# Later side steps in a two-block float32 kernel: the mixer's and the stick-breaking heads', with joined first loads

## The chip, the cores and the metric

One core of one Trainium2 chip runs the whole program. The metric is the device time of one execution in microseconds (us). Three runs of the kernel before gave 2051.86, 2054.35 and 2055.33 us: a median of 2054.35. Lower is better. Everything is float32.

## What is computed

A sequence of 256 rows with 2048 columns goes through two blocks. The first has a state-space mixer, a layer norm, a sparse-attention mixer and a layer norm. The second has an attention of two kinds of heads and an MLP. Only two pieces matter here. The mixer (64 groups of 16 channels, 64 complex states each):

```python
def s5_mixer(x, w_in, ...):
    u, z = jnp.split(x @ w_in, 2, axis=-1)
    ...
    bu_r = jnp.einsum('lbgc,gpc->lbgp', ug, bbar_r)
    _, _, h_r, h_i = lax.associative_scan(_complex_linear_combine, (ar, ai, bu_r, bu_i), axis=0)
    y = einsum('gcp,lbgp->lbgc', c_re, h_r) - einsum('gcp,lbgp->lbgc', c_im, h_i)
    y = y + d_skip * u
    g = jax.nn.gelu(y)
    y = g * jax.nn.sigmoid(g @ w_glu + b_glu)
    return (y * jax.nn.silu(z)) @ w_out
```

And the second block's stick-breaking heads (8 of them, 128 wide):

```python
z = einsum("bqhd,bkhd->bhqk", qb, k) * scale
log_one_minus = jnp.where(strict, jax.nn.log_sigmoid(-z), 0.0)
log_stick = lax.cumsum(log_one_minus, axis=3, reverse=True) - log_one_minus
a = jnp.where(strict, jnp.exp(jax.nn.log_sigmoid(z) + log_stick), 0.0)
out = einsum("bhqk,bkhd->bqhd", a, v)
```

Their outputs are normalised per head, joined with 8 differential heads and multiplied with `w_out` (`co` and `cp` in the profile).

## The kernel before

TensorE (PE) runs one long row of weight chunks. A chunk is a product of the 256 rows with a slice of a weight matrix, 16 k slices of 128 deep, one k slice a step. Beside it go smaller jobs, written as Python generators ("streams"). After each k slice, `step` advances every stream by one, so what a stream does lands between two k slices of the running chunk. `later(n, f)` is a stream that sleeps n steps and then calls f. `drain` runs all streams to their end with nothing between. The instructions go to the engines in the order of the calls, except that a scheduler may still move those not marked `in_order`.

**The mixer.** `u_chunk(b)` (b from 0 to 3) and then `z_chunk(b)` are products with 256 columns of `a_w_in`, full float32, two matmuls (128x256) a k slice (`plain_chunk`, L106 and on; L120). 16 copies on ScalarE (ACT, L394) bring a finished u into `ug`. The states go in four quarters b, each with steps registered by `beside(b)` (L706):

- `b_powers` (L560 to L580, on VectorE, DVE, and ACT's L593): powers of the decay times the input weights, into `ybuf`.
- `states` (L647): 32 PE products `S<-ug,xbuf`, then a DVE chain of 12 pieces from L667 through two scans (L674) to `Hp` (L677, L678).
- `input_weights` (L608): 16 PE transposes `w1t`, four ACT copies (L616) into `W1`.
- `next_c`: the output weights' powers on DVE. `c_blocks` (L600): ACT copies of them into `CP0` and `CPk`.
- `lags` (L621): 32 PE products `tt`, on DVE a copy into `Kl` (L637, L639), then a round trip through DRAM on POOL's queue: `kd` (L642), and four DMAs (L644) into `Tt`.
- `within` (L682): 16 PE products `yb<-ug,Tt`. `outputs` (L690): 32 PE products `yb<-Hp,CPk` into the same bank, then 16 Gelus on ACT (L699).

Between the chunks stands a `drain()`. The buffer `xbuf` holds x (8192 elements a partition: 4096 of x, then W1 and the second CPk). The first chunk's x goes there by 6 DMAs on SyncE's (SP) queue, its weights by 6 DMAs on ACT's queue, into `r_in`.

**The second block.** For each half of the heads, `attend` (L1248) is a stream beside the chunks dv, the queries and keys, `v`, and what follows `v` (`d` in half 0, `co` in half 1). For the stick-breaking heads `weights` is `stick_weights` (scores `sc`, ACT, DVE and POOL, last L1246 on POOL into `lb`). `turned` (L1162) transposes `lb` on PE (`wT`, L1165), `weigh` (L1170) multiplies with the values (`ob`, L1174 to L1176) once the chunk `v` has left PSUM through `sv` (L1151 on ACT, two pieces). `head_out` squares `ob` on ACT, takes a root on DVE, writes `mo` (L1187), transposes it (`moT`, L1193) and stores it as `yH` (ACT) and `yL` (DVE).

Of the kernel before, what the change touches and what calls it, by code (L numbers as in the profile page):

```python
# [17 lines left out]
P = 128  # L18
# [10 lines left out]
def fused_blocks(ctx: ExitStack, tc, ins, out, dbg=None, stages="ABCD"):  # L29
# [318 lines left out]
    with tc.tile_pool(name="pa", bufs=1) as pa:  # L348
# [39 lines left out]
        def u_chunk(b):  # L388
            bank = plain_chunk(ins["a_w_in"][b], xraw, f"u{b}", *((8, 8), space, nc.sync) if b else ((1, 1, 2, 4, 4, 4), first_space, nc.scalar))
# [6 lines left out]
        def z_chunk(b):  # L396
            bank = plain_chunk(ins["a_w_in"][4 + b], xraw, f"z{b}", (8, 8), space, nc.sync)
# [18 lines left out]
        Tt = pa.tile([P, 8, P], F32, name="Tt")  # L416
        G.memset(Tt, 0.0)
# [124 lines left out]
        def rotation(b):  # L542
# [13 lines left out]
               xbuf[:, 6144:8192].rearrange("p (q r k c) -> p q r k c", q=8, r=2, k=4)]  # L556
        for t in CP0 + CPk:
            n = math.prod(t.shape[1:])
            A.copy(t.rearrange("p q r c -> p (q r c)" if len(t.shape) == 4 else "p q r k c -> p (q r k c)"),
                   zero.to_broadcast([P, n]))  # L560
# [39 lines left out]
        def c_blocks(b):  # L600
            cx = cxs[:, b]
            for g in range(2):
                gs, gc = halves(g)
                A.copy(CP0[b % 2][gs, :, :, gc], cx[gs])
                A.copy(CPk[b % 2][gs, :, :, :, gc].rearrange("p q r k c -> p k (q r) c"),
                       Call[gs].rearrange("p k q r c -> p k (q r) c"))

        def input_weights(half):  # L608
            for q2 in (2 * half, 2 * half + 1):
# [6 lines left out]
                A.copy(W1[:, 2 * q2:2 * q2 + 2].rearrange("p q r s -> p (q r s)"), bank)  # L616
# [119 lines left out]
        gHL = big.tile([P, 8, 2, S], F32R, tag="yH", name="gHL")
        gH, gL = gHL[:, :, 0, :], gHL[:, :, 1, :]
        gT = ug.rearrange("p b (m t) -> p (b m) t", m=2)
        for m in range(0, 8, 2):
            A.copy(gH[:, m:m + 2, :], gT[:, m:m + 2, :])  # L740
            V.tensor_sub(gL[:, m:m + 2, :], gT[:, m:m + 2, :], gH[:, m:m + 2, :].bitcast(F32))
        z_chunk(2)
# [7 lines left out]
        for c in range(4):  # L750
            pair = wide_chunk(ins["a_w_glu"][c], (gH, gL, gHL), f"glu{c}")
# [290 lines left out]
    with tc.tile_pool(name="pc", bufs=1) as pc:  # L1042
# [127 lines left out]
        def weigh(wT, v, h, ob):  # L1170
# [3 lines left out]
            T.matmul(ob[:, o:o + P], lhsT=wT[:, 0:128], rhs=v[:, 0, hs], start=(h % 2 == 0), stop=True, skip_group_check=True)  # L1174
# [74 lines left out]
        def attend(weights, q, k, v, norm, k0, gap, wait, first):  # L1249
# [136 lines left out]
def lay_out(i):  # L1386
# [5 lines left out]
    a["xt"] = xt.reshape(P, KD, S)  # L1392
# [18 lines left out]
    a["a_w_in"] = _tiles(i["a_w_in"][0], 8, 256)  # L1411
    a["a_w_glu"] = _tiles(i["a_w_glu"][0], 8, 256)
# [53 lines left out]
```

## Time and profile before

| | us |
|---|---|
| median of three runs | 2054.35 |
| the profiled execution | 2057.24 |
| its span in the trace | 2055.4 |
| PE busy (matmuls) | 2009.5, 98% |
| DVE busy | 1235.4, 60% |
| ACT busy | 935.4, 46% |
| mean granted TensorE clock | 0.991 of full |

The times of instructions count from the start of the span. Busy time is the union of an engine's instructions, so a PE that is 98% busy still may do its work at half the clock: the column PEclk of the windows gives the clock that was granted (1.00 is 2.4 GHz, 0.50 is 1.2 GHz). A full-float32 matmul leaves two records where a cheaper one leaves one. A wait is put down to the semaphore that came last.

### The profile page before, as it was taken

Reading aid. Unit: us, or ns where it says so; the run is one execution under the profiler, and the core shown is the slowest. Engines: PE = TensorE matmul, PEld = TensorE weight load, DVE = VectorE, ACT = ScalarE, POOL = GpSimd, SP = SyncE. Lnnn points to the kernel's source line nnn. Section 1 sums busy time; section 2 is a strip of 40 time slices with the busy share of each in tenths; the row PEclk is TensorE's granted clock in tenths of the full one; section 3 lists DMA queues with packets and bytes.
Section 4 is the critical chain, followed back from the end, with each engine's and each line's share of the span. In section 5 each row is a group of like instructions: output and inputs, shape, how many; then the busy total and the mean of one; then the engine's idle time right before and its main releaser. Section 6 shows DMA issues by size and latency. Waiting matters only on the chain.

```text
span 2055.4 us, 27590 instructions
## 1 busy us (share of the span) xinstructions
PE 2009.5 (98%) x11376; PEld 1708.0 (83%) x11376; DVE 1235.4 (60%) x1802; ACT 935.4 (46%) x1223; POOL 76.0 (4%) x117
## 2 busy tenths in 40 slices
PE   8899999999999999999999999999999999999997
PEld 7788788888888888877878887888888888888886
DVE  8755764466666667567665665565455555555554
ACT  5543543345444545346565565444334334433443
POOL 0110200000000000020010011000000000000000
PEclk9999999999999999999999999999999999999999
DMA  8334554544545454554544544555555555555553
GB/s 313 94 123 153 205 186 166 185 159 167 171 144 175 153 185 144 185 196 176 173 161 144 173 154 154 174 206 185 202 187 186 195 190 187 189 198 186 189 198 124
DMA packets 57119, 361.52 MB, mean 176 GB/s; under 512 B 8481, under 2 KB 9953, under 8 KB 14881
## 3 DMA queue, kind: packets, MB, share of 16 engines
q1 hardware_dynamic: 55296, 355.83, 50.4%
q10 hardware_dynamic: 864, 2.10, 0.3%
q8 instruction: 89, 1.46, 0.3%
q0 software_dynamic: 832, 1.84, 0.3%
q14 instruction: 38, 0.30, 0.0%
HBM read 357.11 MB, written 2.62 MB: 175 GB/s over the span
## 4 chain that ended last, share of the span: by engine, by line
PE 81%; DVE 2%; ACT 2%; issue 1%; POOL 1%; DMA 0%; ACTq 0%; DVEq 0%; POOLq 0%
PE mo L170 17%; PE mi L139 12%; PE bz L139 9%; PE mi L142 6%; PE bz L142 4%; PE bo L170 4%; PE co L170 4%; PE v L170 3%; PE s L139 3%; PE q L139 3%; PE d L170 2%; PE kvv L170 2%; PE kvk L139 1%; PE kvc L139 1%; PE q L142 1%; PE s L142 1%
## 5 line engine op out<-in xcount | busy, mean ns | idle before, releaser
L139 PE MATMUL mi<-hW,h_mi 128*128 128x512 f32 x1024 | 279.5, 394 | 0.0
L103 DVE TENSOR_TENSOR l_mi<-r_mi,h_mi 128x2048 fp32r<-128x2048 f32 x64 | 146.7, 2293 | 152.5 <-ACT h_mi L102 152.5
L103 DVE TENSOR_TENSOR l_mo<-r_mo,h_mo 128x2048 fp32r<-128x2048 f32 x64 | 146.7, 2292 | 149.9 <-ACT h_mo L102 149.9
L139 PE MATMUL bz<-hW,h_bz 128*128 128x512 f32 x768 | 224.3, 412 | 0.0
L102 ACT CAST h_mi<-r_mi 128x2048 fp32r<-128x2048 f32 x64 | 122.3, 1911 | 209.2 <-PE mi L139 166.9
L102 ACT CAST h_mo<-r_mo 128x2048 fp32r<-128x2048 f32 x64 | 122.4, 1913 | 202.9 <-PE mo L170 164.3
L170 PE MATMUL mo<-h_mo,yH 128*128 128x512 f32 x512 | 199.3, 389 | 0.8 <-DVE xres L1366 0.8
L170 PE MATMUL mo<-h_mo,yL 128*128 128x512 f32 x512 | 199.3, 389 | 0.0
L170 PE MATMUL mo<-l_mo,yH 128*128 128x512 f32 x512 | 199.3, 389 | 0.0
L139 PEld LDWEIGHTS mi<-hW,h_mi 128*128 128x128 f32 x1024 | 175.3, 189 | 23.7
L142 PEld LDWEIGHTS mi<-hW,l_mi 128*128 128x128 f32 x1024 | 157.1, 189 | 21.7
L142 PE MATMUL mi<-hW,l_mi 128*128 128x256 f32 x1024 | 163.0, 281 | 0.0
L102 ACT CAST h_bz<-r_bz 128x2048 fp32r<-128x2048 f32 x48 | 91.6, 1909 | 150.3 <-PE bz L139 80.3
L103 DVE TENSOR_TENSOR l_bz<-r_bz,h_bz 128x2048 fp32r<-128x2048 f32 x48 | 110.0, 2292 | 73.7 <-ACT h_bz L102 73.7
L139 PEld LDWEIGHTS bz<-hW,h_bz 128*128 128x128 f32 x768 | 133.5, 189 | 18.4
L142 PEld LDWEIGHTS bz<-hW,l_bz 128*128 128x128 f32 x768 | 117.2, 188 | 16.6
L142 PE MATMUL bz<-hW,l_bz 128*128 128x256 f32 x768 | 121.7, 280 | 0.0
L170 PEld LDWEIGHTS mo<-h_mo,yH 128*128 128x128 f32 x512 | 96.1, 188 | 20.8 <-DVE xres L1366 1.3
L170 PEld LDWEIGHTS mo<-h_mo,yL 128*128 128x128 f32 x512 | 96.1, 188 | 20.1
L170 PEld LDWEIGHTS mo<-l_mo,yH 128*128 128x128 f32 x512 | 96.1, 188 | 20.0
L170 PE MATMUL d<-h_d,hW 128*128 128x512 f32 x256 | 87.6, 415 | 4.6 <-DVE hW L284 2.9
L170 PE MATMUL v<-h_v,hW 128*128 128x512 f32 x256 | 83.3, 397 | 0.0
(509 smaller groups left out, 3783.7 us busy)
## 6 DMA issues: line engine op xcount, KB each, us to landing
r_mi<-in_w_mlp_in SPq DMA_DIRECT2D x64, 1024.0 KB, 4.9
r_mo<-in_w_mlp_out SPq DMA_DIRECT2D x64, 1024.0 KB, 4.9
r_bz<-in_b_w_in SPq DMA_DIRECT2D x48, 1024.0 KB, 4.9
r_q<-in_b_w_in SPq DMA_DIRECT2D x16, 1024.0 KB, 4.9
r_bo<-in_b_w_out SPq DMA_DIRECT2D x16, 1024.0 KB, 4.9
r_d<-in_w_in_2t SPq DMA_DIRECT2D x16, 1024.0 KB, 5.0
r_v<-in_w_in_2t SPq DMA_DIRECT2D x16, 1024.0 KB, 4.8
r_s<-in_w_in_2f SPq DMA_DIRECT2D x16, 1024.0 KB, 4.9
```

Source lines behind the costliest of these rows:

```text
L102: A.copy(wh[:, a:a + w], raw[:, a:a + w])
L103: (eng or V).tensor_tensor(wl[:, a:a + w], raw[:, a:a + w], wh[:, a:a + w].bitcast(F32), op=OP.subtract)
L139: T.matmul(pair[:, m, :], lhsT=wh[:, kk, ms], rhs=aW[:, k, :, :].rearrange("p a t -> p (a t)"), start=(k == 0), stop=(k == kt - 1), skip_g ...
L142: T.matmul(pair[:, m, S:], lhsT=wl[:, kk, ms], rhs=aH[:, k, :], start=False, stop=(k == kt - 1), skip_group_check=True)
L170: T.matmul(banks[t][:, :cols], lhsT=at[:, k, ts_], rhs=wt[:, kk, :], start=(k == 0 and i == 0), stop=(k == kt - 1 and i == 2))
```

## The change

It has five parts.

1. x and the first chunk's weights are one array `xu` (16 k slices of 256 + 256 columns), loaded by 6 DMAs on SP (256 KB twice, 512 KB, 1 MB three times) straight into `xbuf`, now [128, 16, 512]. W1 and the second CPk take the weights' place in it once they are used. The ACT queue issues no load.
2. `Tt` is cleared first, and four products of its zeros (128x256, "still") stand first on PE.
3. The mixer's steps come 8 to 9 k slices later and run on into the next chunk: the drain between chunks is gone, one stands behind `z_chunk(2)`. `b_powers` is a step at 7. `lags(b+1)` now comes between `within(b)` and `outputs(b)`, before it came behind `outputs(b)`. The split of the mixer's result (`gHL`) is a step of `z_chunk(2)`.
4. ACT's copies of the powers and of W1 are pinned with `in_order`, and so is the clearing of the second CPk, now a step. `c_blocks` makes two copies of 64x512 in place of one of 64x1024.
5. The stick-breaking group sleeps two steps more before its first `turned`, four more before its first `weigh`; `turned`'s first transpose and `weigh`'s first product are pinned.

```diff
-        for size in sizes:
-            raw = space(k0, size)
-            in_order(queue.dma_start(raw, w[k0 // kk_n][:, k0 % kk_n:k0 % kk_n + size, :].rearrange("p k c -> p (k c)")))
+        for size in sizes:
+            wt = space(k0, size)
+            if load:
+                in_order(nc.sync.dma_start(wt.rearrange("p k c -> p (k c)"), ...))
...
+        Tt = pa.tile([P, 8, P], F32, name="Tt")
+        G.memset(Tt, 0.0)
+        for _ in range(4):
+            T.matmul(bank_of("pre", "still")[:, 0:256], lhsT=Tt[:, 0, :], rhs=Tt[:, 0:2, :].rearrange("p a b -> p (a b)"),
+                     start=True, stop=True)
...
         def first_space(k0, n):
             ks = slice(k0, k0 + n)
-            fetch(xraw[:, ks, :], ins["xt"][:, ks, :])
-            ...
+            fetch(xbuf[:, ks, :], ins["xu"][:, ks, :])
+            return xbuf[:, ks, S:]
...
+        def clear_second():
+            in_order(A.copy(xbuf[:, 8:16, S:], zero[:, None].to_broadcast([P, 8, 256])))
...
-                A.copy(CP0[b % 2][gs, :, :, gc], cx[gs])
-                A.copy(CPk[b % 2][gs, :, :, :, gc].rearrange("p q r k c -> p k (q r) c"),
-                       Call[gs].rearrange("p k q r c -> p k (q r) c"))
+                in_order(A.copy(CP0[b % 2][gs, :, :, gc], cx[gs]))
+                for r in range(2):
+                    in_order(A.copy(CPk[b % 2][gs, :, r, :, gc].rearrange("p q k c -> p k q c"), Call[gs, :, :, r, :]))
...
-                A.copy(W1[:, 2 * q2:2 * q2 + 2].rearrange("p q r s -> p (q r s)"), bank)
+                in_order(A.copy(xbuf[:, 2 * q2:2 * q2 + 2, S:], bank.rearrange("p (q s) -> p q s", q=2)))
...
         def beside(b):
             if b < 3:
-                b_powers(b + 1)
-            later(1, lambda: states(b))
+                later(7, lambda: b_powers(b + 1))
+            later(9, lambda: states(b))
             if b < 3:
-                later(6, lambda: input_weights(0))
-                later(8, lambda: next_c(b + 1))
-                later(9, lambda: input_weights(1))
-                later(11, lambda: c_blocks(b + 1))
-                later(14, lambda: lags(b + 1))
-            later(10, lambda: within(b))
-            later(13, lambda: outputs(b))
+                later(14, lambda: input_weights(0))
+                later(16, lambda: next_c(b + 1))
+                later(17, lambda: input_weights(1))
+                later(19, lambda: c_blocks(b + 1))
+                later(22, lambda: lags(b + 1))
+            later(18, lambda: within(b))
+            later(22, lambda: outputs(b))
...
         for b in range(4):
-            drain()
             beside(b)
             if b < 2:
                 u_chunk(b + 2)
             else:
                 z_chunk(b - 2)
+        later(10, split_output)
+        z_chunk(2)
         drain()
...
-            yield from sleep(gap)
+            yield from sleep(gap if first else gap + 2)
...
+                if not h and not first:
+                    yield from sleep(4)
                 if h % 2 == 0:
                     ob = small_bank("ob")
                 weigh(wT, v[0], h, ob)
```

What follows on the engines, at three places.

PE, the first quarter from `within(0)` on. `yb<-ug,Tt` is `within`, `yb<-Hp` is `outputs`, `tt` is `lags(1)`; `u` are the chunk's matmuls, here two a k slice. Before:

```order
89 L120 MATMUL u_524<-xbuf,r_in_606 128x256 x2
90 L232 MATMUL yb<-ug,Tt 64x64 [waits DMASW2_49,DMASW1_49]
91 L120 MATMUL u_524<-xbuf,r_in_606 128x256 x2
92 L232 MATMUL yb<-ug,Tt 64x64 [waits DMASW4_49,DMASW3_49]
93 L232 MATMUL yb<-ug,Tt 64x64 x14
94 L120 MATMUL u_524<-xbuf,r_in_606 128x256 x4
95 L232 MATMUL yb<-Hp,CPk 64x64 [waits DVE_49,Pool_49]
96 L232 MATMUL yb<-Hp,CPk 64x64
97 L232 MATMUL yb<-Hp,CPk 64x64 [waits DVE_49]
98 L232 MATMUL yb<-Hp,CPk 64x64 x29
99 L120 MATMUL u_524<-xbuf,r_in_606 128x256 x2
100 L631 MATMUL tt<-CP_299,ybuf 32x32 [waits Activation_49]
```

Now:

```order
94 L617 MATMUL w1t<-ident,ybuf 128x128 [waits Activation_49]
95 L617 MATMUL w1t<-ident,ybuf 128x128 x3
96 L121 MATMUL u_642<-xbuf,r_in_643 128x256 x2
97 L233 MATMUL yb<-ug,Tt 64x64 [waits DMASW2_49,DMASW1_49]
98 L233 MATMUL yb<-ug,Tt 64x64 [waits DMASW4_49,DMASW3_49]
99 L233 MATMUL yb<-ug,Tt 64x64 x14
100 L121 MATMUL u_642<-xbuf,r_in_643 128x256 x8
101 L636 MATMUL tt<-CP_299,ybuf 32x32 [waits PE_49,Activation_49]
102 L640 MATMUL tt<-xbuf,ybuf 32x96 [waits Activation_49]
```

The 32 products `tt` now stand ahead of the 32 products `yb<-Hp`, and 8 matmuls of the chunk instead of 4 to 6 stand between the two kinds of `yb`. Between the last `S` and the first `yb<-ug,Tt` stand 18 chunk matmuls and 16 `w1t` in both.

DVE, from `Kl` of quarter 0 (L639; now L644) to the first piece on `S` (L667; now L672). `rot` and `a` are the rotation, `ybuf`, `bcx` and `ptmp` the powers. Before:

```order
167 L639 SCALAR_TENSOR_TENSOR Kl<-id_165,dT,Kl 128x32 [waits DMAHW4_49,DMAHW1_49,DVE_49]
168 L536 TENSOR_TENSOR a_386<-rot,esg 128x512 [waits DVE_49]
169 L539 TENSOR_TENSOR rot<-rot,esg 128x2x8x32
170 L639 SCALAR_TENSOR_TENSOR Kl<-id_165,dT,Kl 128x32
171 L540 TENSOR_TENSOR rot<-rot,a_386 128x2x8x32 [waits DVE_49]
172 L539 TENSOR_TENSOR rot<-rot,esg 128x2x8x32
173 L667 TENSOR_TENSOR tA<-S_531,rot 128x512 [waits DVE_49,PE_49]
```

Now, from the third piece behind `Kl` on:

```order
174 L582 TENSOR_TENSOR bcx<-bcx,aki 128x32x16
175 L542 TENSOR_TENSOR rot<-rot,a_651 128x2x8x32 [waits DVE_49]
176 L582 TENSOR_TENSOR bcx<-bcx,aki 128x32x16
177 L592 TENSOR_TENSOR ybuf<-bcx,ccr 128x256 [waits Activation_49]
178 L541 TENSOR_TENSOR rot<-rot,esg 128x2x8x32
179 L594 TENSOR_TENSOR ybuf<-ybuf,ptmp 128x256 [waits DVE_49]
180 L541 TENSOR_TENSOR rot<-rot,esg 128x2x8x32
181 L576 TENSOR_TENSOR ybuf<-ybuf,akr 128x768 [waits DVE_49]
182 L582 TENSOR_TENSOR bcx<-ybuf,aki 128x24x16 x2
183 L593 TENSOR_TENSOR ptmp<-bcx,pt_262 128x256
184 L585 TENSOR_TENSOR ybuf<-ybuf,bcx 128x768 [waits DVE_49]
185 L672 TENSOR_TENSOR tA<-S_551,rot 128x512 [waits PE_49]
```

The next quarter's powers, which before stood behind or inside the chain from `S` to `Hp`, now stand ahead of it: 14 pieces between the last `Kl` and the first on `S`. The 12 pieces of the chain itself then follow each other without a piece between.

ACT, where `v` of the stick-breaking heads' half 0 ends. `sv` are the two pieces that empty `v` (L1151; now L1163), `lb` the weights of head 2 (L1245; now L1260). Before:

```order
533 L1151 ACTIVATE sv<-v_8693,rmy 128x512 [waits PE_49]
534 L1245 ACT_TABLE_LOAD
535 L1245 ACTIVATE lb<-lb 128x384 [waits Pool_49]
536 L1151 ACTIVATE sv<-v_8693,rmy 128x512
537 L102 CAST h_d_2_9007<-r_d_2_9005 128x2048 [waits DMAHW7_49]
```

Now:

```order
541 L1163 ACTIVATE sv<-v_8701,rmy 128x512 [waits PE_49]
542 L1163 ACTIVATE sv<-v_8701,rmy 128x512
543 L102 CAST h_d_2_8958<-r_d_2_8956 128x2048 [waits DMAHW1_49]
544 L1260 ACT_TABLE_LOAD
545 L1260 ACTIVATE lb<-lb 128x384 [waits Pool_49]
```

The second piece of `sv` no longer stands behind head 2's exponential, which waits for POOL. On PE the first `wT` of the group moves from 18 matmuls before the end of `v` to 6 before it, and the first `ob` from 6 matmuls behind the end of `v` to 30.

## Rows read from the trace of the kernel before

**Rows 1.** PE's waits over the span; us in total, times, longest.

```profile
PE ob L1176 <- ACT sv L1151: 6.5, 2, 3.7
PE u L120 <- DMA xbuf<-in_xt: 5.3, 2, 4.5
PE wT L1165 <- POOL lb L1246: 3.5, 2, 2.7
PE yb L232 <- DMA Tt<-kd: 3.1, 1, 3.1
PE yb L232 <- DVE Hp L677: 2.3, 1, 2.3
PE w1t L612 <- ACT ybuf L593: 1.6, 1, 1.6
PE ob L1174 <- ACT sv L1151: 1.1, 1, 1.1
```

**Rows 2.** PE timeline from the start: start, us, line, count, idle before.

```profile
4.53 3.85 PE L120 MATMUL u<-xbuf,r_in 128*128 128x256 f32 x8 [4.53 <-DMA xbuf<-in_xt]
9.10 22.51 PE L120 MATMUL u<-xbuf,r_in 128*128 128x256 f32 x92 [0.72 <-DMA xbuf<-in_xt]
```

**Rows 3.** Durations (ns) of the first chunk's matmuls, 10 to 12 us.

```profile
L120 PE MATMUL u<-xbuf,r_in x6: 631/631/631, 9.7 to 11.8; 128*128 128x256 f32 x6
```

**Rows 4.** The same, 12 to 16 us.

```profile
L120 PE MATMUL u<-xbuf,r_in x15: 379/379/631, 11.8 to 15.9; 128*128 128x256 f32 x15
```

**Rows 5.** Windows: PE, PEld, DVE, ACT, POOL busy, PEclk, DMA, GB/s.

```profile
0.00:10.00 10.00, 4.75 (x10) 3.19 (x11) 6.14 (x50) 5.21 (x5) 3.13 (x10) 1.00 0.79 247
10.00:20.00 10.00, 10.00 (x38) 8.30 (x37) 5.48 (x43) 2.18 (x5) 0.00 (x0) 1.00 0.95 343
59.11:66.19 7.08, 7.08 (x44) 5.30 (x45) 7.08 (x13) 0.00 (x0) 0.00 (x0) 0.57 0.01 2
91.53:96.62 5.09, 4.83 (x69) 4.12 (x69) 3.31 (x5) 1.84 (x6) 0.00 (x0) 0.66 0.01 3
1080.43:1086.45 6.02, 6.02 (x16) 4.83 (x17) 2.29 (x1) 1.73 (x1) 0.18 (x1) 0.56 0.19 27
1239.96:1243.20 3.24, 3.24 (x10) 2.68 (x10) 1.47 (x1) 1.74 (x1) 0.17 (x1) 0.56 0.00 0
```

**Rows 6.** POOL timeline at the start.

```profile
0.77 0.95 POOL L417 MEMSET Tt<- 128x1024 f32 x1
```

**Rows 7.** DVE timeline, quarter 0: first and next to last piece from S to Hp.

```profile
49.65 0.67 DVE L667 TENSOR_TENSOR tA<-S,rot 128x512 f32<-128x512 f32 x1
59.28 0.67 DVE L677 TENSOR_TENSOR Hp<-tB,tA 128x512 f32<-128x512 f32 x1
```

**Rows 8.** ACT timeline: the 16 copies that empty a u chunk.

```profile
45.23 4.27 ACT L394 COPY ug<-u 32x128 f32<-32x128 f32 x16
```

**Rows 9.** DMA landings, 60 to 80 us: KB each, us to landing.

```profile
kd<-Kl POOLq DMA_DIRECT2D x1, 128.0 KB, 5.1
Tt<-kd POOLq DMA_DIRECT2D x1, 96.0 KB, 2.6
```

**Rows 10.** DMA landings, 40 to 60 us.

```profile
Tt<-kd POOLq DMA_DIRECT2D x1, 96.0 KB, 6.5
```

**Rows 11.** PE timeline: the chunk's matmuls from the end of tt(0) on.

```profile
39.59 2.86 PE L120 MATMUL u<-xbuf,r_in 128*128 128x256 f32 x12
```

**Rows 12.** POOL timeline, stick-breaking half 1.

```profile
1226.70 2.68 POOL L1244 TENSOR_TENSOR lb<-lb,ck 128x256 f32<-128x256 f32 x1
```

**Rows 13.** ACT timeline, stick-breaking half 1: second piece of sv.

```profile
1239.24 0.67 ACT L1151 ACTIVATE sv<-v,rmy 128x512 f32<-128x512 f32 x1
```

**Rows 14.** PE timeline, last stick-breaking group: last ob, first moT.

```profile
1270.17 0.39 PE L1176 MATMUL ob<-sv,wTs 128*128 128x128 f32 x2
1277.26 0.60 PE L1193 MATMUL moT<-ident,mo 128*128 128x128 f32 x4
```

**Rows 15.** DVE timeline, the same place.

```profile
1274.22 1.12 DVE L1187 SCALAR_TENSOR_TENSOR mo<-ob,hry,hn 128x128 f32<-128x128 f32 x4
```

More of the change, by code (lines that the diff above doesn't have):

```diff
@@ L104, in load, with plain_chunk @@
         return (wh.rearrange("p (k c) -> p k c", c=cols), wl.rearrange("p (k c) -> p k c", c=cols))
-    def plain_chunk(w, x, name, sizes, space, queue):
+    def plain_chunk(w, x, name, sizes, space, load=True):
         _, _, kk_n, cols = w.shape
@@ L388, in u_chunk @@
         def u_chunk(b):
-            bank = plain_chunk(ins["a_w_in"][b], xraw, f"u{b}", *((8, 8), space, nc.sync) if b else ((1, 1, 2, 4, 4, 4), first_space, nc.scalar))
+            bank = plain_chunk(ins["a_w_in"][b], xraw, f"u{b}", *((8, 8), space) if b else ((1, 1, 2, 4, 4, 4), first_space, False))
             for q in range(4):
@@ L555, in fused_blocks @@
         CPk = [pa.tile([P, 8, 2, 4, 32], F32, name="CPk"),
[L556 to L560, printed above, removed]
+               xbuf[:, 8:16, S:].rearrange("p q (r k c) -> p q r k c", r=2, k=4)]
+        for t in CP0:
+            A.copy(t.rearrange("p q r c -> p (q r c)"), zero.to_broadcast([P, 512]))
+        A.copy(CPk[0].rearrange("p q r k c -> p (q r k c)"), zero.to_broadcast([P, 2048]))
+        def clear_second():
+            in_order(A.copy(xbuf[:, 8:16, S:], zero[:, None].to_broadcast([P, 8, 256])))
         Hp = pa.tile([P, 2, 8, 65], F32, name="Hp")
@@ L726, in fused_blocks, with split_output @@
         later(14, lambda: lags(0))
+        later(15, clear_second)
         u_chunk(1)
+        gT = ug.rearrange("p b (m t) -> p (b m) t", m=2)
+        g = []
+        def split_output():
+            gHL = big.tile([P, 8, 2, S], F32R, tag="yH", name="gHL")
+            gH, gL = gHL[:, :, 0, :], gHL[:, :, 1, :]
+            g.extend((gH, gL, gHL))
+            for m in range(0, 8, 2):
+                A.copy(gH[:, m:m + 2, :], gT[:, m:m + 2, :])
+                V.tensor_sub(gL[:, m:m + 2, :], gT[:, m:m + 2, :], gH[:, m:m + 2, :].bitcast(F32))
         for b in range(4):
-            drain()
             beside(b)
@@ L734, in fused_blocks @@
                 z_chunk(b - 2)
+        later(10, split_output)
+        z_chunk(2)
         drain()
[L736 to L742, printed above, removed]
         z_chunk(3)
@@ L750, in fused_blocks @@
         for c in range(4):
-            pair = wide_chunk(ins["a_w_glu"][c], (gH, gL, gHL), f"glu{c}")
+            pair = wide_chunk(ins["a_w_glu"][c], g, f"glu{c}")
             m0 = 2 * c
@@ L1164, in turned @@
             for i in range(3):
-                T.transpose(tb[:, i * P:(i + 1) * P], wt[:, i * P:(i + 1) * P], ident)
+                m = T.transpose(tb[:, i * P:(i + 1) * P], wt[:, i * P:(i + 1) * P], ident)
+                if i == 0:
+                    in_order(m)
             wT = pc.tile([P, 384], F32, tag="wT", name="wTs", bufs=2)
@@ L1173, in weigh @@
             o = h % 2 * S
-            T.matmul(ob[:, o:o + P], lhsT=wT[:, 0:128], rhs=v[:, 0, hs], start=(h % 2 == 0), stop=True, skip_group_check=True)
+            in_order(T.matmul(ob[:, o:o + P], lhsT=wT[:, 0:128], rhs=v[:, 0, hs], start=(h % 2 == 0), stop=True,
+                              skip_group_check=True))
             T.matmul(ob[:, o + P:o + S], lhsT=wT[:, 128:256], rhs=v[:, 0, hs], start=False, stop=False, skip_group_check=True)
@@ L1411, in lay_out @@
     a["a_w_in"] = _tiles(i["a_w_in"][0], 8, 256)
+    a["xu"] = np.concatenate([xt.reshape(P, KD, S), a["a_w_in"][0].transpose(1, 0, 2, 3).reshape(P, KD, 256)], 2)
     a["a_w_glu"] = _tiles(i["a_w_glu"][0], 8, 256)
```

20 lines of the change are left out of this document (7 added, 13 removed).

## The prediction

> **What bounds the kernel now.** I read the page first: PE is busy for 2009.5 of 2055.4 us, so 45.9 us of the span are all that PE stands still, and nothing else can be bound but PE itself. Then PE's waits by what ended them [rows 1]. The reader is to see that six of the seven rows lie in two places that the change touches: the mixer (w1t, both yb) and the stick-breaking heads (wT, both ob), and that the seventh is the start. Then the windows behind the longest waits [rows 5]: PE is busy in them, but its granted clock is 0.56 to 0.66 in the mean, between its two levels of 1.2 and 2.4 GHz. So a long wait is paid twice: for itself, and for the work behind it at half the clock. Waits of about 1 us brought no fall of the clock, those of 2.3 to 3.7 us did. Last the start [rows 2 to 4].
>
> About 0.2% (4 us) is what a measurement of this kernel can tell from no change.
>
> **Mixer waits.** They are 1.6 (w1t, behind an ACT copy), 3.1 (yb on Tt) and 2.3 us (yb on Hp) [rows 1], together 7.0. Behind the second the window of 7.08 us ran at 0.57, so (1 - 0.57) x 7.08 = 3.0 us were lost, behind the third (1 - 0.66) x 5.09 = 1.7 [rows 5]. In all 11.7 us. The change takes their causes away thus:
>
> - w1t waited for a copy that stood behind the 16 copies of u (4.27 us) [rows 8]. w1t stood 6 k slices behind the start of a chunk, now 14.
> - yb on Tt: Tt(0) landed 6.5 us after its issue, while weight loads ran [rows 10]; in the next quarter it was 2.6, though kd took 5.1 [rows 9]. tt(0) stays where it was, within(0) comes 8 k slices later: 8 x 0.92 us = 7.4, more than the 3.1 that lacked. (A k slice is two matmuls, four records; twelve records and the tail of the last take 2.86 us [rows 11].) In the later quarters tt comes earlier against yb, by the 32 products on Hp and one k slice.
> - yb on Hp: the chain of 12 pieces from S takes 59.28 + 0.67 - 49.65 = 10.3 us with three foreign pieces in it [rows 7], some 9.4 without. There is now more PE work between the two kinds of yb: 8 matmuls (3.7 us) and tt (1.1) where 4 to 6 stood.
>
> **What new waits the mixer gets.** Quarter 0 is the tight one. I walk PE through the new order with the durations of the trace: tt(0) ended at 39.59 [rows 11] and now ends 1.3 earlier (the start, below), at 38.3. 22 matmuls (10.1) and S(0) (2.0) follow, so S(0) is done at 50.4. Then 18 matmuls (8.3), w1t (1.8), yb on Tt (1.1), 8 matmuls (3.7) and tt (1.1), so PE wants tt(1) done at 66.3 and then Hp(0). On DVE Kl(0) ends at about 49.6, 14 pieces of powers of 0.33 to 0.87 us follow (about 7.9), then the chain, 9.4: Hp at 66.9. That is 0.6 late. tt(1) wants ACT's copies of c_blocks(1); u2 ends at 56.8, ACT has its 16 copies [rows 8] to about 61.3, two W1 copies, then about 3 us of c_blocks: 65.4 to 65.7, where PE comes at 65.2. I take 1.2 us of new waits in the mixer in all, none long enough for the clock. Bounds: 0 (all hidden), and 13 (the first rival). The larger number of ACT copies in c_blocks costs nothing else: ACT is idle over half of both windows behind the mixer's waits [rows 5]. The clearing of the second CPk moves behind the first chunk on ACT, covered by the same idle time.
>
> **Stick-breaking heads.** The waits are 6.5 + 3.5 + 1.1 = 11.1 us [rows 1], and at half clock behind the two longest (1 - 0.56) x 6.02 = 2.6 and (1 - 0.56) x 3.24 = 1.4 [rows 5], so 15.1. wT waits for POOL, whose piece L1244 took 2.68 us in half 1 [rows 12]; the two more steps of sleep put 12 matmuls (12 x 0.227 = 2.7 us) ahead of wT, as much as its longest wait. The second ob waited for the second piece of sv, which stood behind an exponential that waits for POOL, and in half 1 began at 1239.24 only [rows 13]. Now both pieces stand ahead of that exponential, and PE comes to ob 30 matmuls (6.8 us) after v instead of 6 (1.4). sv needs about 1.4 us in all. I let all 15.1 go; bounds 15.1 and 0 (second rival).
>
> **What is late next.** The whole group ends later, above all the last in half 1: behind its last ob stood 30 matmuls before moT wanted mo [rows 14]. mo was begun 1274.22 - 1270.56 = 3.7 us after the last ob, and the first of its four pieces was ready 0.3 later, at 4.0 [rows 14, 15]. Now 16 matmuls (3.6 us) stand between, then the four transposes with one matmul between each two, and behind 4 more and 12 to 18 others PE wants yH and yL. I put 0.7 us on it; 0 if the scheduler's order hides it, 3 if it turns into a wait that lets the clock fall.
>
> **The start.** Before, PE begins at 4.53, stands 0.72 us for data [rows 2], and its matmuls take 631 ns until 11.8, then 379 [rows 3, 4]: a pitch of 0.46 and of 0.23 us. 14 records fell into the slow part, which cost 14 x 0.23 = 3.2 us. The zero products can begin once Tt is cleared, at 0.77 + 0.95 = 1.7 us [rows 6], and take 8 records of 0.46: to 5.5. Weights and x come by one queue, but need no more than what the traffic gave: 2.47 MB in the first 10 us and 3.43 in the next [rows 5], so 4.2 MB are there at 15, and the chunk's last MB is wanted at 18. After the falls of the clock it took 2.9 to 6.1 us of work until it was full (twice the loss: 2 x 3.24 x 0.44 to 2 x 7.08 x 0.43 [rows 5]), at the start 7.3. From 1.7 on that is 4.6 to 9.0; I take 9.0, the start being the nearest row. Then 7.6 records at the slow pace and 56.4 at the fast end the chunk at 22.0, before at 11.8 + 50 x 0.23 = 23.3. Gain 1.3 us, bounds -0.3 (PE begins later and the clock comes no sooner) and 3.2.
>
> The profile's own column speaks against that gain: it gives a granted clock of 1.00 for the windows 0 to 10 and 10 to 20 us [rows 5], by which the slow matmuls would have another cause and products of zeros would warm nothing. The Trainium skill (TensorE: Matmul & The Clock Gate, Part 1: The HAM clock gate) says that "the default state is throttled, and activity releases the throttle". By the column the term is -0.3, by the rule it is a gain. The durations decide for me: matmuls fall from 631 to 379 ns within one step and keep that, as they do behind each wait where the column does show the fall.
>
> **The sum.** 11.7 + 15.1 + 1.3 - 1.2 - 0.7 = 26.2 us. The profiled execution took 2057.24, so 2031.0 for it. It stands 2.9 above the median of the three runs, so the forecast is 2031.0 - 2.9 = 2028. With the bounds of the start, of the new waits and of the tail it lies between about 2024 and 2034, with 3 us of scatter between runs 2021 to 2036.
>
> **The rivals.**
> - *DVE and ACT become the bound in the mixer.* For it: DVE is busy 7.08 of 7.08 us in the window at 59 [rows 5], and Hp(0) is 0.6 late already by my walk. If each of three quarters has a wait of 2.3 us and a loss of 1.7 behind it, as quarter 1 had, that is 3 x 4.0 = 12 us: 2040. Against it: the powers are ahead of the chain only once a quarter, and DVE has some idle time later.
> - *The stick-breaking shift does not reach.* If POOL and ACT come as much later as PE, the 15.1 stay: 2028 + 15 = 2043. Against it: the scores are not moved, only those who wait for them.
> - *Slower: the pinned row on ACT holds the mixer up.* c_blocks must now stand behind the 16 copies of u and behind W1 copies that wait for PE; tt waits for it, Tt and yb for tt. If in quarters 1 to 3 tt comes late by those 4.3 us [rows 8] and c_blocks' 3, with 3.0 behind it at half clock, that is 3 x 10.3 = 31: 26.2 - 31, slower by 4.7, or 2059. It decides from 26.2 / 3 = 8.7 us a quarter on. Against it: by my walk ACT is 0.5 late, not 7.
> - *The zero products do not do what they are for*: the clock comes up at 11.8 all the same. Then the start gives -0.3 and the time is 2030.
>
> **How the numbers follow.** My forecast 0.60, zero products idle 0.12, mixer bound elsewhere 0.14, shift not reaching 0.09, slower 0.05. The range 2020 to 2041 holds the first two and most of the third, about 0.82. Faster takes all but the last rival and the mixtures of the second and third, 0.92; same 0.03; slower 0.05.
>
> **What would show it.** PE's waits should have none of L1151, L1246 and Tt above 1 us; the granted clock should be 1.00 from 30 to 200 and at both stick-breaking groups; the slow matmuls should end before 9.5 us, and the first glu product should begin some 12 us earlier than before. New rows would be yb on Hp and tt on ACT's copies below 1 us each, and moT or the last co on yL. I am wrong if a wait above 2 us stands in the mixer, or if wT and ob still wait.

## The result

The change takes 2028.95 us (median of four runs, 2028.21 to 2029.94), the kernel before 2054.07 (four runs beside it): a ratio of 0.9878, 95% interval 0.9867 to 0.9890, or 25 us. The forecast was 2028.0, in a range of 2020 to 2041. The profiled execution of the change has a span of 2027.5 us and a mean granted clock of 0.997 (before 0.991). PE is busy for 1998.2 us, 99%.

### The profile page after: what moved, and what is told of

Same layout as the page of the kernel before. It is cut to its first block, busy times and chain, and to the rows that moved or that the text cites. A ratio compares the mean times of both kernels' runs of the same rounds, so it can differ in the third digit from the quotient of the medians.

```text
span 2027.5 us, 27612 instructions
## 1 busy us (share of the span) xinstructions
PE 1998.2 (99%) x11384; PEld 1701.2 (84%) x11384; DVE 1237.4 (61%) x1802; ACT 934.3 (46%) x1231; POOL 80.5 (4%) x117
## 4 chain that ended last, share of the span: by engine, by line
PE 53%; DVE 1%; ACT 0%; issue 0%; DMA 0%; POOL 0%; ACTq 0%; DVEq 0%
PE mo L171 17%; PE mi L140 12%; PE mi L143 6%; PE v L171 4%; PE co L171 4%; PE d L171 4%; PE s L140 3%; PE s L143 1%; PE sc L1169 0%; PE wT L1177 0%; PE sc L1168 0%; DMA r_d<-in_w_in_2t 0%; PE moT L1208 0%; PE dT L1145 0%; PE ob L1191 0%
## 5 line engine op out<-in xcount | busy, mean ns | idle before, releaser
L140 PEld LDWEIGHTS mi<-hW,h_mi 128*128 128x128 f32 x1024 | 175.3, 189 | 23.7
L171 PEld LDWEIGHTS mo<-h_mo,yH 128*128 128x128 f32 x512 | 96.1, 188 | 21.3 <-DVE xres L1383 1.3
L171 PEld LDWEIGHTS mo<-h_mo,yL 128*128 128x128 f32 x512 | 96.1, 188 | 20.0
L171 PEld LDWEIGHTS mo<-l_mo,yH 128*128 128x128 f32 x512 | 96.1, 188 | 19.7
```

Of the source, the lines that this page charges most:

```text
L140: T.matmul(pair[:, m, :], lhsT=wh[:, kk, ms], rhs=aW[:, k, :, :].rearrange("p a t -> p (a t)"), start=(k == 0), stop=(k == kt - 1), skip_g ...
L171: T.matmul(banks[t][:, :cols], lhsT=at[:, k, ts_], rhs=wt[:, kk, :], start=(k == 0 and i == 0), stop=(k == kt - 1 and i == 2))
```

## The profile after

PE's waits in the change, those of the start, the mixer and the stick-breaking heads; the columns are those of [rows 1]:

```profile
PE still L360 <- POOL zero L419: 1.7, 1, 1.7
PE yb L233 <- DVE Hp L682: 1.6, 2, 1.0
...
PE u L121 <- DMA xbuf<-in_xu: 1.4, 2, 0.9
...
PE u L121 <- DMA r_in<-in_a_w_in: 0.6, 1, 0.6
...
PE moT L1208 <- DVE mo L1202: 0.5, 1, 0.5
PE yb L233 <- DVE Hp L683: 0.4, 2, 0.3
```

Of [rows 1], w1t, yb on Tt, wT and both ob are gone. Waits on Hp stay, 2.0 us in all. New are moT (0.5), the products of zeros, which begin as soon as Tt is cleared, and short waits for loads at the start. The windows of the change (columns as in [rows 5]) at the mixer and at the two stick-breaking groups:

```profile
50.00:70.00 20.00, 18.86 (x236) 16.28 (x233) 19.86 (x29) 13.07 (x31) 3.12 (x6) 1.00 0.27 89
70.00:90.00 20.00, 20.00 (x255) 17.21 (x255) 17.32 (x27) 13.57 (x43) 3.12 (x6) 1.00 0.39 129
1057.00:1070.00 13.00, 13.00 (x64) 10.90 (x63) 7.01 (x7) 10.12 (x13) 6.08 (x10) 1.00 0.41 156
1209.00:1219.00 10.00, 10.00 (x49) 8.19 (x48) 6.21 (x6) 9.28 (x11) 4.04 (x7) 1.00 0.64 211
```

The granted clock, which was 0.56 to 0.66 behind the waits of before [rows 5], is 1.00, and in three of the four PE never stands still. DVE is the busiest beside it from 50 to 70: 19.86 of 20 us.

Where the time went is read from the first instruction of each stage, change against before. The timeline of PE at the end of the mixer, before and then after:

```profile
168.39 0.81 PE L139 MATMUL glu<-gHL,h_glu 128*128 128x512 f32 x2
```

```profile
156.00 1.27 PE L140 MATMUL glu<-gHL,h_glu 128*128 128x512 f32 x4
```

The first glu product begins 12.4 us sooner. In half 0 the first v begins 11.8 sooner (970.9, now 959.1), the last d 20.8 (1131.0, now 1110.2): 9.0 us from that group. In half 1 the first co comes 23.5 sooner (1235.3, now 1211.8), the last 27.6 (1335.4, now 1307.8): 2.7 at wT, then 4.1 more. Behind that 0.3 us more come over the rest of the span. So in these two profiles the mixer with the start gave 12.4 and the heads 15.8. The profiled execution of the kernel before lies 3.2 us above its median, so this pair overstates the gain: the kernel of experiment 2, whose mixer is the old one, begins its first glu product at 164.7, 8.7 us behind the change.

## The experiments

Each kernel is the change with the edit shown, unless another is named. "Slower" is against the median of the change, 2028.95; an interval is that of the ratio to the kernel before, run on the same chip. The kernel before had medians of 2053.5 to 2054.4 beside these runs, so a difference of about 1 us is not told apart.

**1. The heads as before.** The diff takes out `+ 2`, `sleep(4)` and the two pins of part 5.

> The change without its fifth part: no extra sleep in the stick-breaking groups, nothing pinned there. In the program's order wT stands again 18 matmuls before the end of v, ob 6 behind it, and head 2's exponential between the two pieces of sv. Theory (the shift of these groups is worth the waits 11.1 us and the 4.0 us at half clock that it takes away, less 0.5 us that moT now waits): about 14.5 us slower than the change, 2043.5, with waits on wT (0.8 and 2.7) and on ob (1.1, 3.7, 2.7) and the granted clock near 0.56 behind the two longest. Rival (the heads' waits went because everything ahead of them moved): under 3 us slower, 2029 to 2032.

2043.39 us (2042.38 to 2044.51), interval 0.9934 to 0.9964: 14.4 slower, as the theory said. PE's waits in this run:

```profile
PE ob L1188 <- ACT sv L1163: 6.4, 2, 3.7
PE wT L1177 <- POOL lb L1258: 3.5, 2, 2.7
...
PE ob L1186 <- ACT sv L1163: 1.1, 1, 1.1
```

All three are those of before to 0.1 us, though everything ahead of them had moved by 12 us. The expectation also had the clock near 0.56 behind the two longest waits of ob; only one shows a fall. Behind the 3.7 us of half 0 it was 0.62 over 6.0 us (2.3 lost). Behind the 2.7 us of half 1 it stayed at 1.00, where the same wait of 2.7 us in the kernel before was followed by 0.56 [rows 5]. PE there, and its window (columns as in [rows 5]):

```profile
1227.56 0.49 PE L1188 MATMUL ob<-sv,wTs 128*128 128x128 f32 x2 [2.73 <-ACT sv L1163]
```

```profile
1227.56:1230.80 3.24, 3.24 (x15) 2.75 (x16) 1.47 (x1) 1.74 (x1) 0.17 (x1) 1.00 0.02 5
```

**2. The heads alone, on the kernel before.** Part 5 is put into the kernel before, nothing else.

> The kernel before with the change's fifth part alone: the two steps ahead of wT, the four ahead of ob, and the pinned first instructions. Theory (the parts add up: this one is worth the 14.4 us that its removal cost): 2054.1 - 14.4 = 2039.7, no wait on wT or ob, and the mixer's waits (1.6, 3.1, 2.3) as before. Rival (its gain needs the other parts): under 12 us faster, over 2042.

2039.02 us (2037.43 to 2042.59) against 2053.48, interval 0.9920 to 0.9947: 14.5 us faster. Taken out or put in, this part is worth the same within the scatter (the interval of this run is 11 to 16 us), so no dependence on the other parts is seen. The mixer kept its waits (1.7, 2.9, 2.3). But the clock behind the wait for Tt stayed at 1.00. PE at that wait, and the window behind it, as long as the one at 59.11 in [rows 5]:

```profile
58.26 0.30 PE L232 MATMUL yb<-ug,Tt 128*64 128x64 f32 x2 [2.90 <-DMA Tt<-kd]
```

```profile
58.26:65.34 7.08, 7.08 (x112) 5.91 (x112) 7.08 (x13) 0.64 (x3) 0.00 (x0) 1.00 0.01 3
```

From the end of the wait PE reached yb on Hp in 4.3 us here (62.55), in 7.1 us in the profile of before (66.19). So the 3.0 us at half clock behind Tt are not lost in every execution of the old mixer.

**3. Without the two steps ahead of wT.**

```diff
-            yield from sleep(gap if first else gap + 2)
+            yield from sleep(gap)
```

> The change with only the two steps ahead of the first wT taken back; the four ahead of the first ob stay. wT stands 18 matmuls before the end of v, ob 30 behind it, and head 2's exponential stands again between the two pieces of sv. Theory (each wait belongs to its own distance on PE): wT waits 0.8 and 2.7 us, some 1.4 us at half clock behind the longer one, ob waits under 0.5: 4 to 5 us slower than the change, 2033.5. Rival A (it is the place of the exponential that makes the waits of ob): ob waits 2 to 4 us more in each half and the clock falls in both, 2038 to 2043. Rival B (the two steps do nothing): 2029.

2036.42 us (2034.07 to 2038.10), interval 0.9894 to 0.9928: 7.5 slower, more than the 4.5 expected. PE's waits:

```profile
PE wT L1177 <- POOL lb L1261: 3.5, 2, 2.7
...
PE ob L1188 <- ACT wTs L1181: 2.1, 1, 2.1
```

wT waits as expected, and here the clock behind its longest wait falls (0.81 over the 8 us from 1214, so 1.5 us lost). No ob waits for sv, although head 2's exponential stands between its two pieces again: rival A is out. What I had missed is the third wait. It is in half 0, at the second `ob`, on ACT's copy of wT, which stands behind a cast of d's weights that landed late:

```profile
1067.59 3.71 ACT L102 CAST h_d<-r_d 128x2048 fp32r<-128x2048 f32 x2
1077.37 1.90 ACT L102 CAST h_d<-r_d 128x2048 fp32r<-128x2048 f32 x1 [6.07 <-DMA r_d<-in_w_in_2t]
1079.17 0.47 ACT L1181 COPY wTs<-wT 128x384 f32<-128x384 f32 x1
```

ACT stood still 6.07 us for the load, and behind PE's wait the clock was 0.64 over 4.7 us (1.7 lost). 3.5 + 1.5 + 2.1 + 1.7 = 8.8, the whole difference of the two spans (2036.3 and 2027.5); this profile is of the slowest of the four runs, so the others may have had less of it. Why the load came late was not tried. A guess from the order: the two casts ahead of it had come back to back, which moves the time at which the loads' buffers come free.

**4. Without the four steps ahead of ob.**

```diff
-                if not h and not first:
-                    yield from sleep(4)
```

> The change with only the four steps ahead of the first ob taken back; the two ahead of wT stay. ob stands 6 matmuls behind the end of v as before the change, but both pieces of sv stand ahead of head 2's exponential on ACT. Theory (it was the exponential between the two pieces that made the long waits of ob, 24 matmuls of distance only cover what is left): sv needs 1.4 us after v and PE comes after 1.4 us, so ob waits 0.3 to 1.0 us in each half with the clock at 1.00, and moT no longer waits: 2029 to 2030.5. Rival (the distance is what takes the waits away): ob waits 2 us and more in each half, the clock falls: 2034 to 2038.

2034.81 us (2034.18 to 2035.48), interval 0.9892 to 0.9922: 5.9 slower. The theory was wrong, the rival right, half 1 being milder. PE's first ob in half 0 and in half 1, and ACT ahead of the first of them:

```profile
1064.43 0.80 PE L1188 MATMUL ob<-sv,wTs 128*128 128x128 f32 x2 [2.15 <-ACT sv L1163]
...
1219.01 0.49 PE L1188 MATMUL ob<-sv,wTs 128*128 128x128 f32 x2 [1.41 <-ACT sv L1163]
```

```profile
1058.75 1.89 ACT L102 CAST h_d<-r_d 128x2048 fp32r<-128x2048 f32 x1
1060.55 0.47 ACT L1181 COPY wTs<-wT 128x384 f32<-128x384 f32 x1
1060.91 0.50 ACT L1241 ACTIVATE l<-sc 128x384 f32<-128x384 f32 x1
1061.44 0.53 ACT L1242 ACTIVATE l<-l 128x384 f32<-128x384 f32 x1
1061.98 1.28 ACT L1243 ACT_TABLE_LOAD   x1
1063.28 0.52 ACT L1243 ACTIVATE l<-l 128x384 f32<-128x384 f32 x1
1063.71 1.25 ACT L1163 ACTIVATE sv<-v,rmy 128x512 f32<-128x512 f32 x2
```

The two pieces of sv take 1.25 us and stand together, ahead of the exponential, and still PE waits. ACT is busy without a gap: sv stands behind a cast of d's weights, the copy of wT and head 2's first chain (three pieces and a table load), which follows the copy of wT. So the distance from wT to ob on PE has to cover the copy, that chain and sv; from the copy of wT to the end of sv it is 4.4 us. The cast holds that copy back by 1.7 us more (wT ends at 1058.87); what the wait would be without it was not tried. From 1064.43 to 1070.00 the granted clock was 0.70, 1.7 us lost; behind the 1.41 us it stayed 1.00. 2.15 + 1.41 + 1.7 - 0.5 (moT no longer waits) = 4.8 of the 5.9.

**5. Two steps instead of four ahead of ob.** `sleep(4)` becomes `sleep(2)`.

> The change with two steps ahead of the first ob in place of four: ob stands 18 matmuls behind the end of v. In the run without any of them ob waited 2.15 us in half 0 and 1.41 in half 1, because sv stands on ACT behind head 2's first chain, which begins with wT. Theory (the distance from wT to ob must cover that chain and no more): 12 matmuls are 2.7 us, more than 2.15, so no wait on sv above 0.3 in either half and the clock stays at 1.00; the last group ends 12 matmuls sooner, so moT's wait of 0.5 us is gone: 2028.0 to 2029. Rival (the waits move with the distance, as sv is held up by other casts): waits of 1 us and more stay, 2030 to 2033.

2030.41 us (2030.12 to 2031.19), interval 0.9876 to 0.9903: 1.5 slower, a miss. The runs don't overlap with the change's, though the intervals do. As the theory had it no ob waits for sv, the clock at both groups is 1.00, and 12 matmuls suffice for sv. But the profile loses elsewhere: from the first v to the last d of half 0 it takes 152.3 us (957.5 to 1109.8), the change 151.1; from the first to the last co 97.0 against 96.0. The 1.0 of half 1 is found again in experiment 12 (96.9), the other run with two steps, and in no profile with four (96.0 to 96.1). The 1.2 of half 0 is not shown to come from the edit: experiment 8, with the heads of the change, takes 152.1 there too. A part of half 1's is seen at the four transposes of mo for half 1's first pair of heads, in this run and in the change:

```profile
1235.77 1.01 PE L1208 MATMUL moT<-ident,mo 128*128 128x128 f32 x4
```

```profile
1238.39 0.60 PE L1208 MATMUL moT<-ident,mo 128*128 128x128 f32 x4
```

They now come as mo's pieces do, too close behind ob. What the rest is stays open.

**6. The mixer's steps as before.** `beside` gets the old numbers and `b_powers` at once, the drains come back, the split stands behind the drain; loads, zeros, pins and heads stay.

> The change with the mixer's steps where they were (states at 1, input weights at 6 and 9, c_blocks at 11, lags at 14, within at 10, outputs at 13, a drain before each quarter, the split of the result behind the drain). First loads, zero products, pinned copies and stick-breaking groups stay as in the change. Theory (the later steps take away waits of 7.0 us and 4.7 us at half clock, and bring 2.0 us of waits on Hp): 9 to 10 us slower than the change, about 2038.5, with waits on w1t, Tt and Hp of 1.5 to 3 us and the granted clock below 0.7 behind the two longest. Rival (the pinned order of ACT's copies did it): the waits stay small, 2030 to 2032. Rival (pinned copies hurt in the old order): over 2042.

2036.39 us (2036.23 to 2038.49), interval 0.9902 to 0.9932: 7.4 slower, two less than expected. PE in quarter 0:

```profile
48.15 0.66 PE L617 MATMUL w1t<-ident,ybuf 128*128 128x128 f32 x4 [0.48 <-DVE Kl L642]
...
58.19 0.35 PE L233 MATMUL yb<-ug,Tt 128*64 128x64 f32 x2 [5.06 <-DMA Tt<-kd]
59.10 1.94 PE L233 MATMUL yb<-ug,Tt 128*64 128x64 f32 x30 [0.56 <-DMA Tt<-kd]
```

The wait for Tt is back and longer, and the window from 58.2 to 66.0 ran at 0.56 (3.4 us lost). Those on w1t (1.6, now 0.5) and Hp (2.3, now none) did not come back. So the later steps, with the drains gone, are what hides the round trip of Tt; the other two waits are gone in this kernel without them, with pins and start in place.

**7. ACT's copies not pinned.** `in_order` is taken off the copies of `c_blocks` and of W1.

> The change with ACT's copies in c_blocks and of W1 no longer pinned; the scheduler then puts the copies of CP and CPk for a quarter further ahead, in front of the copies of u. Theory (the pinned copies are covered by ACT's idle time and PE waits for Hp, not for them): within 1 us of the change, 2028 to 2030. Rival A (pinning holds tt and Hp up): 1 to 2 us faster. Rival B (without pins the early copies push back what PE waits for first, as w1t did in the kernel before): a wait of 1 us or more on w1t, S or ug in several quarters, 3 to 10 us slower.

2034.22 us (2032.75 to 2034.73), interval 0.9887 to 0.9916: 5.3 slower. Rival B is right in size, but the wait is on Hp. PE in quarter 0, and DVE ahead of it:

```profile
69.10 0.34 PE L233 MATMUL yb<-Hp,CPk 128*64 128x64 f32 x4 [3.51 <-DVE Hp L682]
```

```profile
58.65 0.67 DVE L672 TENSOR_TENSOR tA<-S,rot 128x512 f32<-128x512 f32 x1
...
64.49 0.39 DVE L593 TENSOR_TENSOR ptmp<-bcx,pt 128x256 f32<-128x256 f32 x1
...
65.94 0.67 DVE L582 TENSOR_TENSOR bcx<-bcx,aki 128x512 f32<-128x512 f32 x1
...
67.68 0.67 DVE L582 TENSOR_TENSOR bcx<-bcx,aki 128x512 f32<-128x512 f32 x1
68.28 0.67 DVE L682 TENSOR_TENSOR Hp<-tB,tA 128x512 f32<-128x512 f32 x1
```

In the change the chain begins at 57.33 and Hp at 65.81; here at 58.65 and 68.28. ACT makes the copies of CPk for quarter 1 at 37.23 already (change 61.99). With the powers' buffer free so early, two larger pieces (L576, L585, 1.21 us each), which stood behind Hp in the change, stand ahead of the chain on DVE, and the three shown land inside it. The pins of ACT's copies are felt on DVE. The profile is of the fastest of the four runs: its first glu product begins at 160.0, 4.0 us later than the change's, of which 2.5 are the longer waits on Hp and 1.2 the clock behind them (0.70 over 4.0 us from 69).

**8. Without the products of zeros.** The loop over `still` is taken out.

> The change without the four products of zeros; Tt is still cleared first. Theory (the products bring the clock up before the first data land): the chunk's matmuls begin near 4.2 us, take 631 ns each until 10 to 11.5 us and 379 ns after; 13 or so records at the slow pace cost 3 us, of which PE's waits for data in the change (1.4 us) would have taken a part anyway, so the first chunk ends 0.8 to 1.6 us later than in the change and the time is 2029.5 to 2030.7. Rival (the slow matmuls at the start have nothing to do with what PE did before): the pace turns at the same moment as in the change, 5.4 us, the chunk ends no later and the time is 2028 to 2029.

2029.87 us (2028.41 to 2032.82), interval 0.9869 to 0.9898: the runs overlap with the change's, no difference shown. PE at the start, of the change and then of this run:

```profile
1.75 3.78 PE L360 MATMUL still<-Tt 128*128 128x256 f32 x8 [1.75 <-POOL zero L419]
5.32 2.39 PE L121 MATMUL u<-xbuf 128*128 128x256 f32 x8
8.62 1.99 PE L121 MATMUL u<-xbuf 128*128 128x256 f32 x8 [0.91 <-DMA xbuf<-in_xu]
11.12 10.63 PE L121 MATMUL u<-xbuf 128*128 128x256 f32 x48 [0.51 <-DMA xbuf<-in_xu]
```

```profile
3.99 3.38 PE L121 MATMUL u<-xbuf 128*128 128x256 f32 x8 [3.99 <-DMA xbuf<-in_xu]
8.68 1.99 PE L121 MATMUL u<-xbuf 128*128 128x256 f32 x8 [1.31 <-DMA xbuf<-in_xu]
11.17 10.63 PE L121 MATMUL u<-xbuf 128*128 128x256 f32 x48 [0.50 <-DMA xbuf<-in_xu]
```

With or without them the third load lets PE go on at 8.6 and the fourth at 11.1. Both end the first chunk at 21.8; the loads set it, not the pace of the matmuls ahead of them. The time lies in the range of the theory, but its reason, a first chunk that ends later, is not there.

**9. The zeros on the kernel before.** Tt is cleared first there too, and the four products are added.

> The kernel before, with Tt cleared first and the four products of zeros ahead of its first chunk, nothing else. Its first chunk ran 14 records at the slow pace until 11.8 us. Theory (the products bring the full pace to the first chunk here too, but the next loads then bound PE): the matmuls take 379 ns from 5.5 to 7.5 us on, the first chunk ends 1 to 2.5 us sooner, PE then waits up to 1 us for the second chunk's weights; 2051.5 to 2053.5 against 2054.2. Rival (nothing is won, since the loads bound the first chunk in any case): 2054 to 2055.

2053.58 us (eleven runs, 2050.85 to 2056.73) against 2053.48, interval 0.9994 to 1.0012: nothing. The durations of the first chunk's matmuls in this run (columns as in [rows 3]), up to 7 us and from 7.5:

```profile
L120 PE MATMUL u<-xbuf,r_in x4: 631/632/632, 5.3 to 6.6; 128*128 128x256 f32 x4
```

```profile
L120 PE MATMUL u<-xbuf,r_in x11: 379/380/454, 7.3 to 10.7; 128*128 128x256 f32 x11
```

The full pace comes at 7.2 us, before at 11.8 [rows 3, 4] and in experiment 2, with the same start as before, at 12.3; so the products do what they are for. PE then waits 1.0 and 1.3 us for x, and w1t waits 0.8 us: it begins at 31.57, where ACT's copy of the powers ends at 31.47. S of quarter 0 begins at 42.53, before at 42.38 and in experiment 2 at 41.67.

**10. Finer first loads.** `(1, 1, 2, 4, 4, 4)` becomes `(1, 1, 1, 1, 2, 2, 2, 2, 2, 2)`.

> The change with its first loads cut finer: 1, 1, 1, 1, 2, 2, 2, 2, 2, 2 k slices in place of 1, 1, 2, 4, 4, 4. Theory (PE, already at the full clock at 5.4 us, now waits for whole pieces of 512 KB and 1 MB to land: 0.9 and 0.5 us): the waits spread out and shrink, the first chunk ends 0.3 to 1.0 us sooner, 2028.0 to 2028.7. Rival (the rate of the traffic bounds it, not the piece): the chunk ends at the same 21.7 us or later, because ten issues on SP take longer than six: 2029 to 2030.

2029.78 us (2028.74 to 2030.40), interval 0.9866 to 0.9896. The rival is right in the time, not in the place:

```profile
5.32 14.72 PE L121 MATMUL u<-xbuf 128*128 128x256 f32 x64
22.65 9.72 PE L121 MATMUL u<-xbuf,r_in 128*128 128x256 f32 x36 [2.61 <-DMA r_in<-in_a_w_in]
```

The first chunk runs through without a wait and ends 1.7 us sooner, at 20.0, and PE stands 2.61 us for the second chunk's weights: it goes on at 22.65 against 22.30 in the change. Behind that wait the clock was 0.68 over 5.3 us (1.7 lost), so the first tt begins at 39.23 against 37.20; by the first glu product 0.6 of the 2.0 us are left, as the waits on Hp shrink from 2.0 to 0.9. The loads of the first 22 us are the bound: whichever piece comes first, PE waits until then for the second chunk.

**11. Outputs one slice later.** `later(22, ...)` of `outputs` becomes 23.

> The change with outputs one k slice later (23 for 22). Theory (Hp is late by 1.0 + 0.2 us in quarter 0 and 0.6 + 0.3 in quarter 3, and a k slice of 0.92 us covers most of it): waits on Hp fall from 2.0 to under 0.5 us, 2027.2 to 2028. Rival (the end of the chain is set by what is behind outputs, Gelu and the split of the result, or by tt): what is won at Hp comes back as a wait on S, ug or glu: 2029.

2028.39 us (2027.46 to 2029.49), interval 0.9860 to 0.9893. The waits on Hp fall from 2.0 to 1.0 us and the first glu product comes at 154.6 (change 156.0). But 1.0 of these 1.4 us were there before any output: the first tt begins at 36.24, in the change at 37.20. The runs overlap with the change's: not shown to be faster.

**12. Outputs later, and two steps instead of four.**

> The change with outputs one k slice later (23) and two steps in place of four ahead of the first ob. Theory (the two savings are independent: some 1.4 us by the first glu product, and 0.5 us of moT's wait): 2027 to 2028, 1 to 2 us faster than the change. Rival (what is saved is lost in a later wait): 2029.

2030.93 us (2030.27 to 2031.50), interval 0.9877 to 0.9908: 2.0 slower. The rival is right in direction, and the time lies above even its 2029; it carries the loss of experiment 5. No version that beats the change beyond its scatter was found.

## Why the prediction was right

**The heads: right, with one step wrong and the last 0.1 us by luck.** Forecast 15.1 less 0.7 for moT, 14.4 us. Taking the part out cost 14.4, putting it in alone gave 14.5. That agreement is closer than the scatter of the runs, and the term of 1.4 for the clock in half 1 was not there when experiment 1 brought the wait back. moT waited 0.49, its first transpose standing alone:

```profile
1252.37 0.30 PE L1208 MATMUL moT<-ident,mo 128*128 128x128 f32 x1 [0.49 <-DVE mo L1202]
```

Long waits, and in half 0 a half clock behind the longest, are what the part is about: the waits alone sum to 11.1, and the part is worth 14.4. The wrong step is "sv needs about 1.4 us in all". sv's own 1.25 us are right, but experiment 4 shows it behind 2.8 us of head 2's chain on ACT, so the distance of 24 matmuls that I took for a reserve is needed in part: without it PE lacks 2.15 us, and half of it takes the waits on sv away (experiment 5). With the exponential between the pieces, which I gave as the reason, the wait is longer (3.7 us in experiment 1, 2.15 in 4, though the two differ in the steps ahead of wT and the pins as well), but the distance covers it too (experiment 3).

**The mixer: right in sum, wrong in whom it credits.** Forecast with the start 11.7 + 1.3 - 1.2 = 11.8; in the profiles 12.4, in the medians 25.1 - 14.4 = 10.7. I gave the whole 11.7 to the later steps. With all else in place they are worth 7.4 (experiment 6), and the pins, for which the sum has no term, 5.3 (experiment 7). The two don't add: each is what is lost when it alone is taken away. ACT's idle time covered the pinned copies, as I had it; that the pins also set DVE's order was not in the working.

**The clock: right in sum, too simple as a rule.** I read that waits of about 1 us brought no fall of the clock and those of 2.3 to 3.7 did, and counted 4.7 us in the mixer and 4.0 in the heads for it. The trace I read from has an exception: wT's longest wait of [rows 1], 2.69 us, with the clock at 1.00 behind it:

```profile
1230.12:1234.12 4.00, 4.00 (x21) 3.44 (x21) 2.29 (x1) 3.95 (x5) 0.71 (x2) 1.00 0.55 229
```

And the same wait at the same place brings a fall in one execution and none in another. Behind Tt 3.0 us were lost in the profile of before, 1.7 in experiment 9 (0.76 over 7.1 us) and none in experiment 2; behind half 1's ob 1.4 before and none in experiments 1 and 9. So the profile I summed from was an execution with more falls than others, and it lay 2.9 us above the median. I took 26.2 off that profile and then 2.9 more, as if the change would keep this excess. The pair of profiles shows otherwise: the change gave 27.9 of span, 1.7 more than the sum, and its profiled execution, 2029.30, lies only 0.35 above its median. The two errors nearly cancel. That the forecast came within 1 us is luck to that extent; by the sum alone it would have been 2031.

**New waits.** Forecast 1.2, measured 2.0 on Hp: 0.97 + 0.17 in quarter 0, 0.59 + 0.27 in quarter 3, none of which lowered the clock. The walk had quarter 0 late by 0.6, with Hp ready at 66.9; DVE wrote its second half from 66.42 on, to 67.10. tt did not wait for ACT's copies. The first rival's condition, 2.3 us a quarter, was reached by experiment 7 alone, and there in one quarter.

**The start: right in size, not by the way I gave.** Forecast 1.3, from a rise of the clock at 9.0. It came at about 6, earlier than that, and what it won went into waits for loads (0.91 + 0.51 + 0.55). The first tt begins at 37.20, before at 38.47 and in experiment 2, with the old start, at 37.76: 1.3 and 0.6 us sooner. Experiments 8 and 9 show no gain for the products of zeros, so the term belongs to the joined loads if to anything; they were not tried alone. Of the fourth rival the reason is refuted (the pace did turn earlier), its time was not told apart. The profile's column, 1.00 while matmuls took 631 ns, was the wrong one to trust. Experiment 9, where the pace turned at 7.2 us behind products of zeros and not at 11.8, agrees with the rule of the Trainium skill weighed there (TensorE: Matmul & The Clock Gate, Part 1: The HAM clock gate).

**The slower rival** had the pinned copies holding the mixer up. They hold it together: without them it is slower.

## What to carry to other kernels

Look at the clock behind a wait of the busiest engine as well as at the wait, then move the consumer later by what the producer lacks. The waits can be summed from rows; what the clock costs behind them differs between executions, so take it from more than one profile before it goes into a sum. What the producer lacks is counted on the queue of the engine that makes it, from the event that starts that queue (here wT), not from the producer's own duration. A pin on one engine changes what the scheduler does on another, so look at the order of both; and ahead of a stretch that is bound by loads, neither a faster clock nor finer pieces gave time here.

## What the runs showed that was not expected

- The column of the granted clock reads 1.00 throughout the first 20 us, while matmuls of one shape take 631 ns and then 379. The durations have to be read there.
- Without zeros the full pace came at 11.8 us in the kernel before, but at 7.0 in experiment 8, where PE began at 3.99 and ran its first eight records without a gap. The kernel before ran its first eight without a gap too, from 4.53 on [rows 2]. Why the rise came 3.0 us behind the first matmul in one and 7.3 in the other stays open. The moment of the rise can't be carried from one kernel to another.
- The length of a wait alone does not tell whether the clock falls behind it. Waits of 2.1 to 2.7 us were followed by a fall in experiments 3 and 4 and one of 1.4 was not, but 2.73 (experiment 1) and 2.90 (experiment 2) were not either. In the change's own profile PE waits 2.88 us for `hW` in a chunk d, to 905.7, and the clock stays at 1.00; before, it was 0.57 over the 4 us behind the same wait (2.86). Then PE waits 1.08 us, to 912.5, and the clock is 0.69 over the next 5.5. What else decides was not tried.
- With the same first loads, the second chunk began between 21.3 and 23.7 us in the profiles of these runs: more than any edit of the start moved.
